# The u products' input in PSUM, the latents' sums in the scores' banks, and all of the context's v rows on VectorE

## The chip, the core and the metric

The kernel runs on one core of one Trainium2 chip. The metric is the time of one execution on the device in microseconds (us); less is better. A core has TensorE (PE in the profile; its weight loads are PEld), VectorE (DVE), ScalarE (ACT), GpSimd (POOL) and SyncE (SP), which run their own instruction streams side by side and wait for each other by semaphores. SBUF is the working memory; PSUM is the memory that TensorE writes its products to, here eight banks of 512 float32 per partition.

## What is computed

The reference is a two-layer diffusion backbone over 256 latent tokens and 256 context tokens of width 1024. Each layer mixes tokens (two attentions, a convolution, a pooling, four gated branches) and then runs a retrieval network on every token:

```
def chunk(xc):                      # 128 tokens
    q = (xc @ wq).reshape(128, 8, 2, 128)
    ...                             # top 16 of 256 candidates for each of 8 heads
    gate = softmax(sc)
    u = jnp.take(u_tab, idx, axis=0)                    # 128 rows of 1024 for each token
    act = gelu(jnp.einsum('td,thkd->thk', xc, u))
    v = jnp.take(v_tab, idx, axis=0)                    # another 128 rows
    return jnp.einsum('thk,thkd->td', gate * act, v)
```

So every token needs 128 rows of `u_tab`, a dot product with each, and a weighted sum of 128 rows of `v_tab`; all is float32. The context is needed only up to the first layer's end, so there are six chunks of 128 tokens: two of context (layer 1), two of latents (layer 1), two of latents (layer 2).

## The kernel before

A chunk is a tile of 128 tokens, one on each partition. Its gather runs over j = 0 to 127; for each j, `u_slot` has GpSimd issue an indirect DMA (line 1124) that brings one row of `u_tab` for each of the 128 tokens (512 KB), and VectorE multiplies it with the tile's input `h2` and sums along the row (line 1132, a scalar_tensor_tensor of 128x1024, "the u product"). Sixteen j make a group; after it, ScalarE and VectorE turn the group's 16 dot products into weights. `v_slot`, one group behind, issues the DMA of a v row and adds weight times row to a sum: either on VectorE into the SBUF tile `dacc` (line 1149, "the v sum"), or on TensorE, where ScalarE first makes a diagonal matrix `dg` of the weights (line 1154) and two float32 matmuls of 512 columns add the row to `va`, two PSUM banks (line 1156). At the end `add` (lines 1170, 1171) scales each sum and adds it to the residual `X`.

The six gathers run in this order, and the text calls them so: C0 (context, first tile), L0 and L1 (latents, layer 1), C1 (context, second tile), F0 and F1 (latents, layer 2). Which j's v rows VectorE sums is set by a rule for each (line 1272): C0 all but 6, L0 and F0 every fourth, L1 and F1 every second, C1 three in four but one. C0 runs beside the latents' token mixer of layer 1 and C1 beside that of layer 2: their rows are put between the mixer's products as `pump` gives them credit, in program order. L0, L1 and F1, and F0 after its first rows, run with nothing large beside them but the router of their neighbour, whose selections of the top 16 are VectorE's.

The rows land in places: SBUF buffers, 5 for u and 5 for v beside the mixers, 12 and 9 with those lent in layer 1's latents (`lend`). GpSimd waits where no place is free. `h2` is made by `prepare` (lines 1102 to 1113) from `X`, a scale and two rows that TensorE spreads over the partitions in PSUM tiles `tr`. `va` is one PSUM tile of two banks; `at`, two tiles of one bank each, holds the attentions' scores; `mm` and `tr` take the other four banks. Each engine's instructions stand in the order that a scheduler gave them at build time, and run in it.

## Time and profile before

| | us |
|---|---|
| median of 3 runs | 3176.56 |
| lowest, highest | 3165.32, 3186.99 |
| the profiled execution | 3168.74 |
| its span, first to last instruction | 3167.0 |

| engine | busy, us | share of the span |
|---|---|---|
| PE (matmul) | 2376.9 | 75% |
| DVE | 2357.8 | 74% |
| POOL | 1789.3 | 56% |
| ACT | 654.6 | 21% |

The profile is of one execution. A group of instructions is named by its line, engine and operation and by "output<-inputs" (an `h` there is `h2`, `u,act` the u product's outputs). [...] The indirect rows are 805.40 of the 1036.48 MB that the kernel moves. "issue" is time in which an engine waited for nothing that the profile shows.

### The profile page before, as it was taken

Reading aid. Unit: us, or ns where it says so; the run is one execution under the profiler, and the core shown is the slowest. Engines: PE = TensorE matmul, PEld = TensorE weight load, DVE = VectorE, ACT = ScalarE, POOL = GpSimd, SP = SyncE. Lnnn points to the kernel's source line nnn. Section 1 sums busy time; section 2 is a strip of 40 time slices with the busy share of each in tenths; the row PEclk is TensorE's granted clock in tenths of the full one; section 3 lists DMA queues with packets and bytes.
Section 4 is the critical chain, followed back from the end, with each engine's and each line's share of the span. In section 5 each row is a group of like instructions: output and inputs, shape, how many; then the busy total and the mean of one; then the engine's idle time right before and its main releaser. Section 6 shows DMA issues by size and latency. Waiting matters only on the chain.

```text
span 3167.0 us, 32196 instructions
## 1 busy us (share of the span) xinstructions
PE 2376.9 (75%) x10264; PEld 1586.2 (50%) x10264; DVE 2357.8 (74%) x5204; ACT 654.6 (21%) x1543; POOL 1789.3 (56%) x1542
## 2 busy tenths in 40 slices
PE   7999989898877785665455589899997966645555
PEld 5879878666666452222111267667696522211111
DVE  5977679678968899747666769977567985566666
ACT  3454321233112211110000211123332211100001
POOL 0000057443556687776777757766205777777775
PEclk9999999899988897886777789899998988876767
DMA  9948979787999899998999999999838989999998
GB/s 305 334 161 285 304 263 351 270 296 250 339 331 356 321 392 364 336 381 294 373 369 369 338 343 389 341 388 386 300 107 288 323 324 372 372 344 372 383 377 300
DMA packets 397863, 1036.48 MB, mean 327 GB/s; under 512 B 30464, under 2 KB 169216, under 8 KB 397696
## 3 DMA queue, kind: packets, MB, share of 16 engines
q0 software_dynamic: 221184, 805.40, 68.0%
q1 hardware_dynamic: 173072, 226.25, 21.0%
q10 hardware_dynamic: 3440, 2.78, 0.3%
q8 instruction: 82, 1.34, 0.2%
q14 instruction: 85, 0.70, 0.1%
HBM read 1032.22 MB, written 2.10 MB: 327 GB/s over the span
## 4 chain that ended last, share of the span: by engine, by line
PE 33%; DVE 18%; issue 17%; DMA 15%; POOL 15%; ACT 1%; another core or an unknown queue 0%; POOLq 0%; SPq 0%; ACTq 0%; DVEq 0%
PE mm L218 11%; POOL u L1124 8%; POOL v L1124 7%; DMA v<-in_v_dram,idx 7%; DVE u L1132 5%; PE va L1156 4%; DMA w<-in_w_gate_dram 3%; PE mm L214 3%; PE mm L216 2%; PE mm L215 2%; PE mm L916 2%; DMA u<-in_u_dram,idx 2%; DVE dacc L1149 2%; PE at L531 2%; DVE m L832 2%
## 5 line engine op out<-in xcount | busy, mean ns | idle before, releaser
L1124 POOL DMA_INDIRECT u<-in_u_dram,idx x768 | 869.7, 1132 | 926.4 <-DVE m L862 409.0
L1156 PE MATMUL va<-v,dg 128*128 128x512 f32 x1436 | 890.5, 763 | 554.5 <-DMA v<-in_v_dram,idx 379.8
L1132 DVE SCALAR_TENSOR_TENSOR u<-u,h 128x1024 f32<-128x1024 f32 x768 | 933.2, 1219 | 338.1 <-DMA u<-in_u_dram,idx 307.6
L1124 POOL DMA_INDIRECT v<-in_v_dram,idx x768 | 919.1, 1197 | 433.6 <-issue 193.9
L1156 PEld LDWEIGHTS va<-v,dg 128*128 128x128 f32 x1436 | 315.8, 237 | 1070.4 <-issue 925.6
L1149 DVE SCALAR_TENSOR_TENSOR dacc<-v,wt,dacc 128x1024 f32<-128x1024 f32 x403 | 515.6, 1279 | 105.9 <-DMA v<-in_v_dram,idx 78.6
L218 PE MATMUL mm<-hT,w 128*128 128x256 f32 (+1 forms) x1664 | 383.4, 385 | 71.4 <-DMA w<-in_w_gate_dram 50.9
L218 PEld LDWEIGHTS mm<-hT,w 128*128 128x128 f32 x1664 | 312.4, 207 | 130.2 <-issue 53.6
L1154 ACT ACTIVATE dg<-ident,wt 128x128 f32<-128x128 f32 x359 | 141.3, 400 | 1029.9 <-PE va L1156 524.7
L832 DVE SCALAR_TENSOR_TENSOR m<-m,cols,m 128x256 f32<-128x256 f32 x360 | 158.2, 473 | 0.1
L916 PE MATMUL mm<-hT,w 128*128 128x256 f32 x512 | 134.5, 405 | 14.5 <-DVE t L453 6.6
L215 PE MATMUL mm<-hT,whi 128*128 128x256 f32 x512 | 143.4, 280 | 0.0
L214 PE MATMUL mm<-hT,whi 128*128 128x256 f32 x448 | 128.0, 286 | 3.1 <-ACT whi L176 3.1
L216 PE MATMUL mm<-hT,whi 128*128 128x256 f32 x448 | 127.2, 284 | 1.8 <-DVE whi L177 1.8
L218 PE MATMUL mm<-w,hT 128*128 128x256 f32 x512 | 117.1, 388 | 10.6 <-DMA w<-in_w_in_dram 10.6
L916 PEld LDWEIGHTS mm<-hT,w 128*128 128x128 f32 x512 | 97.6, 202 | 34.5 <-issue 17.2
L177 DVE TENSOR_TENSOR whi<-w,whi 128x1024 fp32r<-128x1024 f32 x86 | 103.6, 1220 | 13.8 <-ACT whi L176 6.5
L218 PEld LDWEIGHTS mm<-w,hT 128*128 128x128 f32 x512 | 99.1, 195 | 26.4 <-issue 12.5
L176 ACT CAST whi<-w 128x1024 fp32r<-128x1024 f32 x86 | 87.4, 1047 | 51.3 <-PE mm L216 20.6
L215 PEld LDWEIGHTS mm<-hT,whi 128*128 128x128 f32 x512 | 97.0, 190 | 0.4 <-issue 0.3
L214 PEld LDWEIGHTS mm<-hT,whi 128*128 128x128 f32 x448 | 85.3, 190 | 8.8 <-ACT whi L176 4.2
L216 PEld LDWEIGHTS mm<-hT,whi 128*128 128x128 f32 x448 | 84.8, 189 | 7.2 <-DVE whi L177 3.7
(361 smaller groups left out, 2960.9 us busy)
## 6 DMA issues: line engine op xcount, KB each, us to landing
w<-in_w_gate_dram SPq DMA_DIRECT2D x48, 1024.0 KB
w<-in_w_in_dram SPq DMA_DIRECT2D x42, 1024.0 KB
X<-in_w_mod_dram SPq DMA_DIRECT2D x40, 512.0 KB
wm<-in_w_mod_dram SPq DMA_DIRECT2D x40, 512.0 KB
w<-in_w_branch_dram SPq DMA_DIRECT2D x20, 1024.0 KB
w<-in_w_q_dram SPq DMA_DIRECT2D x20, 1024.0 KB
u<-in_u_dram,idx POOLq DMA_INDIRECT x768
v<-in_v_dram,idx POOLq DMA_INDIRECT x768
```

Of the source, the lines that this page charges most:

```text
L177: nc.vector.tensor_tensor(lo.bitcast(FR), v, hi, op=OP.subtract)
L214: nc.tensor.matmul(ps, ah, bh, start=first, stop=False)
L215: nc.tensor.matmul(ps, ah, bl, start=False, stop=False)
L216: nc.tensor.matmul(ps, al, bh, start=False, stop=last)
L218: nc.tensor.matmul(ps, a[:, kb, ca], b[:, kb, cb], start=first, stop=last)
L832: nc.vector.scalar_tensor_tensor(acc[:, b, :], yb[:, b, k:k + T], cols[:, l, cw + k:cw + k + 1], acc[:, b, :], op0=OP.mult, op1=OP.add)
L916: nc.tensor.matmul(ps, a[:, kb, ca], b[:, k0 + kb, cb], start=f, stop=z, skip_group_check=True)
L1124: nc.gpsimd.indirect_dma_start(out=r, out_offset=None, in_=table, in_offset=bass.IndirectOffsetOnAxis(ap=self.idx[:, j:j + 1], axis=0))
L1132: nc.vector.scalar_tensor_tensor(r, r, 1.0, self.h2, op0=OP.mult, op1=OP.mult, accum_out=self.act[:, j % 16:j % 16 + 1])
L1149: nc.vector.scalar_tensor_tensor(self.dacc, v, w, self.dacc, op0=OP.mult, op1=OP.add)
L1154: nc.scalar.activation(dg, ident, AF.Copy, scale=w)
L1156: nc.tensor.matmul(self.va[:, half, :], dg, v[:, half * 512:(half + 1) * 512], start=j == self.pe[0], stop=j == self.pe[-1])
```

## The change

`prepare` computes `h2` in SBUF as before up to its last step; for a tile of latents (t > 1) the last addition writes into a PSUM tile of the tag `va`, and the u products read that. The tile's sums on TensorE go to two tiles of the tag `at`. A context tile has no rows on TensorE any more: `self.pe` is empty, VectorE sums all 128, and `add` runs once. The rules for C0 and C1 fall away.

```
         def prepare(self, found=False):
 
-            self.h2 = sb.tile([128, D], F, tag="h2", name="h2", bufs=2)
+            h2 = sb.tile([128, D], F, tag="h2", name="h2", bufs=2)
+
+            self.h2 = va_ps() if self.t > 1 else h2
             if found:
-                nc.vector.tensor_copy(self.h2[:, ::512], self.idx[:, :2])
+                nc.vector.tensor_copy(h2[:, ::512], self.idx[:, :2])
             for half in range(2):
                 c = slice(half * 512, (half + 1) * 512)
                 ps = bcast(tr_ps(), A[self.l][1][:, self.s, half * 4:half * 4 + 4])
-                nc.vector.scalar_tensor_tensor(self.h2[:, c], X[:, self.t, c], rst2[:, self.t:self.t + 1], ps,
+                nc.vector.scalar_tensor_tensor(h2[:, c], X[:, self.t, c], rst2[:, self.t:self.t + 1], ps,
                                                op0=OP.mult, op1=OP.mult)
                 ps = bcast(tr_ps(), modc[self.l][:, self.s, 24 + half * 4:28 + half * 4])
-                nc.vector.tensor_tensor(self.h2[:, c], self.h2[:, c], ps, op=OP.add)
+                nc.vector.tensor_tensor(self.h2[:, c], h2[:, c], ps, op=OP.add)
 
         def begin(self, on_dve):
 
-            self.pe = [j for j in range(128) if not on_dve(j) or j >= 128 - LAST]
+
+            self.pe = [j for j in range(128) if not on_dve(j) or j >= 128 - LAST] if self.t > 1 else []
             self.dv = [j for j in range(128) if j not in self.pe]
-            self.va = va_ps().rearrange("p (a b) -> p a b", a=2)
+            self.va = [at_ps() for half in range(2)] if self.pe else None
...
-                    nc.tensor.matmul(self.va[:, half, :], dg, v[:, half * 512:(half + 1) * 512],
+                    nc.tensor.matmul(self.va[half], dg, v[:, half * 512:(half + 1) * 512],
                                      start=j == self.pe[0], stop=j == self.pe[-1])
...
-        t.add(t.va.rearrange("p a b -> p (a b)"))
+        if t.pe:
+            t.add(t.va)
...
-    P_C0, P_L0, P_L1, P_C1, P_F0, P_F1 = (lambda j: j < 48 or (j * 15) % 16 < 15), few, half, most, few, half
+    P_L0, P_L1, P_F0, P_F1 = few, half, few, half
...
-    behind.append(gather(tsc[0], P_C0, None, rc))
+    behind.append(gather(tsc[0], None, None, rc))
...
-    behind.append(gather(tsc[1], P_C1))
+    behind.append(gather(tsc[1], None))
```

Line numbers of the changed kernel are higher by 2 to 4 (the u product is line 1135 there, the v sum 1152, `add` 1173 and 1174, `prepare` 1112 and 1115).

VectorE at the hand-over from L0 to L1, before: L0's last v sums, its two `add`s (the sum in `dacc`, then the one in `va`) and L1's first u products, with L1's input `h_9901`, which was made earlier.

```order
L1149 SCALAR_TENSOR_TENSOR dacc<-v,wt,dacc 128x1024 x4
L1170 TENSOR_TENSOR dacc<-dacc,g_9926 128x512 x2
L1171 TENSOR_TENSOR X<-X,dacc 128x512 x2
L1132 SCALAR_TENSOR_TENSOR u,act<-u,h_9901 128x1024
L1170 TENSOR_TENSOR dacc<-va,g_9926 128x512 x2
L1171 TENSOR_TENSOR X<-X,dacc 128x512 x2
L1132 SCALAR_TENSOR_TENSOR u,act<-u,h_9901 128x1024 x5
```

And now (`h_9880` is L1's input before its last step, `h_11154` that of C1):

```order
L1135 SCALAR_TENSOR_TENSOR u,act<-u,va 128x1024 x3
L1115 TENSOR_TENSOR va<-h_9880,tr 128x512
L1142 TENSOR_TENSOR wt<-wt,gate 128x16
L1115 TENSOR_TENSOR va<-h_9880,tr 128x512
L1152 SCALAR_TENSOR_TENSOR dacc<-v,wt,dacc 128x1024 x2
L1112 SCALAR_TENSOR_TENSOR h_11154<-X,few_cols,tr 128x512
L1152 SCALAR_TENSOR_TENSOR dacc<-v,wt,dacc 128x1024
L1115 TENSOR_TENSOR h_11154<-h_11154,tr 128x512
L1152 SCALAR_TENSOR_TENSOR dacc<-v,wt,dacc 128x1024
L1173 TENSOR_TENSOR dacc<-dacc,g_9906 128x512 x2
```

The single tile `va` is written for L1 right behind L0's last u product; nothing else of the order at this place is new but C1's `prepare`, which moved up by a few instructions.

VectorE in C1, beside the convolution of layer 2 (line 832, a chain of 128x256 operations), before:

```order
L1132 SCALAR_TENSOR_TENSOR u,act<-u,h_11173 128x1024
L832 SCALAR_TENSOR_TENSOR m_11926<-m_11425,cols,m_11926 128x256
L1132 SCALAR_TENSOR_TENSOR u,act<-u,h_11173 128x1024
L832 SCALAR_TENSOR_TENSOR m_11926<-m_11425,cols,m_11926 128x256
L1149 SCALAR_TENSOR_TENSOR dacc<-v,wt,dacc 128x1024
```

And now:

```order
L1135 SCALAR_TENSOR_TENSOR u,act<-u,h_11154 128x1024
L832 SCALAR_TENSOR_TENSOR m_11888<-m_11405,cols,m_11888 128x256
L1152 SCALAR_TENSOR_TENSOR dacc<-v,wt,dacc 128x1024
L832 SCALAR_TENSOR_TENSOR m_11888<-m_11405,cols,m_11888 128x256
L1135 SCALAR_TENSOR_TENSOR u,act<-u,h_11154 128x1024
```

Every u product is now followed by a v sum. From the convolution's first instruction in C1 to its last there stood 27 v sums on VectorE and stand 34 now.

TensorE at the end of that stretch (line 916: the gates' products; `t_`: transposes of the attention's inputs; line 796: the convolution's statistics), before:

```order
L218 MATMUL mm<-w,hT 128x256 x13
L1156 MATMUL va<-v,dg 128x512 x2
L916 MATMUL mm<-hT,w 128x256
L463 MATMUL tr<-ident,t_12309 128x128 x4
L916 MATMUL mm<-hT,w 128x256 x14
L463 MATMUL tr<-ident,t_12372 128x128 x4
L916 MATMUL mm<-hT,w 128x256 x9
L1156 MATMUL va<-v,dg 128x512 x2
L796 MATMUL tr<-few_cols,m_11926 128x1 x3
```

And now:

```order
L218 MATMUL mm<-w,hT 128x256 x15
L916 MATMUL mm<-hT,w 128x256
L463 MATMUL tr<-ident,t_12256 128x128 x4
L916 MATMUL mm<-hT,w 128x256 x14
L463 MATMUL tr<-ident,t_12316 128x128 x4
L916 MATMUL mm<-hT,w 128x256 x9
L796 MATMUL tr<-few_cols,m_11888 128x1 x3
```

The context's v rows are gone from TensorE's order; the mixer's products stand as before.

## Rows read from the trace of the kernel before

**Rows 1.** The page's head: span and number of instructions.
```profile
span 3167.0 us, 32196 instructions
```
**Rows 2.** Stretches: us, busy (count) of PE, PEld, DVE, ACT, POOL; clock, DMA share, GB/s.
```profile
400.00:1000.00 600.00, 504.63 (x2342) 409.35 (x2342) 492.76 (x1110) 135.40 (x318) 318.91 (x256) 0.91 0.86 307
1040.00:1280.00 240.00, 175.50 (x499) 95.16 (x498) 235.46 (x781) 45.15 (x106) 186.38 (x151) 0.85 0.96 360
1280.00:1406.00 126.00, 83.55 (x160) 33.37 (x160) 77.09 (x137) 17.15 (x43) 98.59 (x86) 0.82 0.95 347
1440.00:1783.00 343.00, 190.93 (x286) 67.95 (x287) 230.92 (x332) 31.61 (x82) 264.48 (x242) 0.71 0.97 366
1784.00:2260.00 476.00, 414.05 (x1804) 314.12 (x1802) 371.08 (x652) 100.10 (x248) 323.77 (x256) 0.92 0.96 357
2440.00:2600.00 160.00, 126.53 (x414) 72.15 (x413) 153.50 (x503) 35.71 (x84) 110.02 (x96) 0.92 0.88 313
2600.00:2784.00 184.00, 123.52 (x231) 48.43 (x232) 93.29 (x138) 24.07 (x60) 134.36 (x129) 0.83 0.97 368
2790.00:3150.00 360.00, 185.61 (x249) 60.21 (x248) 239.66 (x342) 29.52 (x76) 272.87 (x252) 0.70 0.97 368
```
**Rows 3.** Waits in 1440 to 1783: us in total, times, longest.
```profile
POOL v L1124 <- issue: 36.3, 119, 0.3
...
DVE u L1132 <- DMA u<-in_u_dram,idx: 76.6, 57, 2.7
```
**Rows 4.** Timeline in F1: start, duration, engine, line, operation [idle before].
```profile
2899.78 0.94 POOL L1124 DMA_INDIRECT u<-in_u_dram,idx  x1 [0.30 <-issue]
...
2900.94 1.22 DVE L1132 SCALAR_TENSOR_TENSOR u<-u,h 128x1024 f32<-128x1024 f32 x1 [2.37 <-DMA u<-in_u_dram,idx]
2901.02 1.95 POOL L1124 DMA_INDIRECT v<-in_v_dram,idx  x1 [0.31 <-issue]
```
**Rows 5.** Timeline at the start of L1, beside `prepare`'s operation with a PSUM input.
```profile
1440.46 0.74 DVE L1110 SCALAR_TENSOR_TENSOR h<-X,few_cols,tr 128x512 f32<-128x512 f32 x1
1440.50 0.93 POOL L1124 DMA_INDIRECT u<-in_u_dram,idx  x1 [0.30 <-issue]
```
**Rows 6.** Line 1132 alone in L0's end, L1, F1: DVE busy (count); clock, DMA.
```profile
1280.00:1406.00 126.00, 52.14 (x86) 0.82 0.95 347
1440.00:1783.00 343.00, 150.26 (x246) 0.71 0.97 366
...
2790.00:3150.00 360.00, 157.25 (x256) 0.70 0.97 368
```
**Rows 7.** Line 1149 alone in the same stretches.
```profile
1280.00:1406.00 126.00, 16.67 (x13) 0.82 0.95 347
1440.00:1783.00 343.00, 78.36 (x61) 0.71 0.97 366
...
2790.00:3150.00 360.00, 78.32 (x61) 0.70 0.97 368
```
**Rows 8.** A stretch of F1, all engines.
```profile
3040.00:3080.00 40.00, 23.30 (x33) 7.52 (x32) 28.21 (x40) 3.02 (x8) 30.58 (x31) 0.74 1.03 408
```
**Rows 9.** Two lines: duration ns min/median/max, first and last start, form.
```profile
L1110 DVE SCALAR_TENSOR_TENSOR h<-X,few_cols,tr x12: 720/740/749, 414.4 to 2549.9; 128x512 f32<-128x512 f32 x12
...
L304 DVE SCALAR_TENSOR_TENSOR msum<-wm,silc,msum x28: 733/744/748, 106.8 to 353.7; 128x512 f32<-128x512 f32 x28
```
**Rows 10.** The page's group of line 1149: count | busy us, mean ns | idle before, releaser.
```profile
L1149 DVE SCALAR_TENSOR_TENSOR dacc<-v,wt,dacc 128x1024 f32<-128x1024 f32 x403 | 515.6, 1279 | 105.9 <-DMA v<-in_v_dram,idx 78.6
```
**Rows 11.** Two stretches of C1, all engines.
```profile
1920.00:2045.00 125.00, 108.47 (x431) 82.56 (x431) 121.19 (x225) 11.75 (x27) 93.71 (x66) 0.89 0.97 356
2045.00:2260.00 215.00, 207.70 (x959) 153.85 (x957) 151.96 (x247) 67.60 (x169) 141.09 (x118) 0.97 0.97 370
```
**Rows 12.** Line 1156 alone in the second of them: PE busy (count), PEld busy (count).
```profile
2045.00:2260.00 215.00, 32.38 (x64) 12.18 (x64) 0.97 0.97 370
```
**Rows 13.** The chain that ended last, in the same stretch, by line.
```profile
by line: PE mm L916 30.6%; DMA v<-in_v_dram,idx 14.8%; PE va L1156 10.6%; PE tr L218 9.7%; PE at L531 8.8%; PE tr L557 7.7%; DMA w<-in_w_gate_dram 5.5%; issue 4.6%; PE tr L553 3.9%; POOL v L1124 1.5%; POOL u L1124 1.1%; PE tr L1176 0.9%; PE
```

More of the change, by code (lines that the diff above doesn't have):

```diff
@@ L1150, in v_slot @@
                 if j == self.dv[-1]:
-                    self.add(self.dacc)
+                    self.add([self.dacc[:, :512], self.dacc[:, 512:]])
             else:
@@ L1169, in add @@
                 c = slice(half * 512, (half + 1) * 512)
-                nc.vector.tensor_tensor(self.dacc[:, c], v[:, c], self.g2[:, c], op=OP.mult)
+                nc.vector.tensor_tensor(self.dacc[:, c], v[half], self.g2[:, c], op=OP.mult)
                 nc.vector.tensor_tensor(X[:, self.t, c], X[:, self.t, c], self.dacc[:, c], op=OP.add)
```

## The prediction

> **What bounds the kernel now.** I first read the busy times by stretch, cut where a gather begins or ends and where its router stops [rows 2]. The kernel has no single bound. From 400 to 1000 us (C0) and from 1784 to 2260 (C1) the mixers' products on TensorE share the core with a gather. The stretches 1040 to 1280 (most of L0) and 2440 to 2600 (the first part of F0) carry the router's selections, and VectorE is busy for 235.46 of 240 and 153.50 of 160 us: it sets their time. Four stretches are left in which only a gather runs: 1280 to 1406 (L0's end), 1440 to 1783 (L1), 2600 to 2784 (F0's end) and 2790 to 3150 (F1), together 1013 us, a third of the span [rows 1].
>
> In these four no compute engine is full: VectorE is busy 51 to 67%, TensorE 52 to 67%. The DMA engines show a share of 0.95 to 0.97 and would pass for the bound. The second view, GpSimd's waits, says otherwise. Between two of its indirect DMAs lie 36.3/119 = 0.305 us of "issue", a wait for nothing shown, and hardly any other wait [rows 3]. L1 has 242 of them: 264.48 busy + 242 x 0.305 = 338 of 343 us. F1: 272.87 + 76.9 = 350 of 360. F0's end: 134.36 + 39.3 = 174 of 184; L0's end: 98.59 + 26.2 = 125 of 126 [rows 2]. GpSimd is never free there, and VectorE waits for its rows (76.6 us in L1) [rows 3]. It is the bound: a row costs its instruction's time plus 0.305 us.
>
> The third view is the timeline, for how long that instruction takes. Beside an idle VectorE it takes 0.94 us. One that starts 0.08 us after a u product, which reads two tensors from SBUF, takes 1.95: the product ends at 2900.94 + 1.22 = 2902.16, and the DMA instruction 0.81 us later [rows 4]. Beside an operation of the same kind whose second tensor is in PSUM (`prepare`'s line 1110), it takes 0.93 [rows 5]. So GpSimd stands still behind a VectorE operation with two SBUF tensors, and not behind one with a PSUM tensor. For the latents the change turns the first into the second.
>
> **The cost of each part.** (1) The waits of GpSimd in the four stretches. Over 0.94 us an instruction: L0's end 98.59 - 86 x 0.94 = 17.8 us; L1 264.48 - 227.5 = 37.0; F0's end 134.36 - 121.3 = 13.1; F1 272.87 - 236.9 = 36.0 [rows 2]; in all 104. They stand behind u products and v sums, which both read two SBUF tensors; I split them by the busy times of the two: u products have 52.14 of 68.81 in L0's end, 150.26 of 228.62 in L1, 157.25 of 235.57 in F1 [rows 6, 7], so 76, 66 and 67%; for F0's end, with L0's rule for v rows, 76%. That makes 13.5 + 24.3 + 9.9 + 24.0 = 72 us behind u products and 32 behind v sums. The 72 fall away. But GpSimd then comes round sooner and meets v sums that it missed while it stood behind a u product: I let the 32 grow by a third, by 11. Net 61, and as GpSimd fills 97% of these stretches, 59 us. The bounds: 72 if the v sums catch no more than now, about 20 if they catch most of it. A row would then cost 1.34 us in place of 1.42; 1.29 us a row and less is seen already, in 40 us of F1 with 31 rows at 408 GB/s [rows 8], so the transfers can follow.
>
> (2) The same waits where VectorE is the bound: 186.38 - 141.9 = 44 us in L0's first stretch, 20 in F0's [rows 2]. VectorE idles there for only 4.5 and 6.5 us, so GpSimd merely fills its places earlier; of the 11 us I take 5. Bounds: 0, and 15 with what the filled places save behind the selections.
>
> (3) The u product from PSUM. No row shows a 128x1024 one. The nearest are the 128x512 operations of the same kind, 740 ns with a PSUM input and 744 without [rows 9]: no difference, so 0. [...]
>
> (4) The context's v rows. VectorE gets 6 + 33 = 39 v sums of 1.279 us [rows 10], 50 us, and loses two second `add`s. In C1 it is full from 1920 to 2045 (121.19 of 125) [rows 11], beside the convolution; 7 of the new sums fall there by the order: 9 us on the path. From 2045 to 2260 TensorE is full (207.70 of 215) [rows 11] and VectorE is not; the v rows take 32.38 us of TensorE [rows 12] and, with their transfers that it waits for in order, 25% of the chain, some 55 us [rows 13]. All that goes, but the transfers run at 370 GB/s already [rows 11]: at about 400, between that and the 408 of rows 8, the stretch would be 199 us, 16 less; I take 14. So C1 gains 5; bounds: 9 lost, 15 gained. In C0, 6 rows change engine, and neither engine is full (505 and 493 of 600) [rows 2]: 0, at worst 6 x 1.28 = 8 us.
>
> (5) `va` and `at`. The order writes `va` for the next tile right behind the last u product on the same engine, and the sums' tiles are handed on by the `add`, as `va` was: 0. Were the input late, 16 u products of the first group would be queued behind it, and with them GpSimd once its places are full: a few us at each of four hand-overs.
>
> Sum: -59 - 5 + 0 - 5 = -69 us against the profiled execution's 3168.74 (its span of 3167.0 and 1.7 around it): 3100. The median of the runs is 7.8 above that execution: 3107.
>
> **The rivals.** *The transfers are the bound.* For it: the DMA share of 0.95 to 0.97 [rows 2]. Then GpSimd's gain only lengthens the queue, and 3% of 1013 us, 30, is all there is: 3147. Against it: 408 GB/s where GpSimd was rarely held [rows 8]. [...] *The v sums take over.* VectorE runs v sums in 13% (L0's end) to 23% (L1) of a stretch [rows 7]; if GpSimd falls into step with them, only part (1)'s lower bound of 20 comes, with (2) and (4) 30: 3147. For it: half the rows of L1 and F1. *The PSUM operand doesn't free GpSimd*, because something else about the products holds it: only (4), 3172. Against it: rows 5, in the same kind of operation. *All waits shrink.* If fewer collisions also break up those behind v sums, 72 + 15 + 15 = 102 and more: 3070. *The other side: C1 starves.* With 128 v sums, u products and the convolution all reading two SBUF tensors, GpSimd may find no gap; it waits 83 us in C1 now and uses 402 of 476 with the pauses [rows 2]. Its time must pass 476 before this costs anything; and for the kernel to be slower by 1% C1 must grow by 64 (the gain of (1) and (2)) + 32 = 96 us. VectorE alone does not do it: 371 + 42 = 413 of 476 [rows 2]. Every wait would have to triple: 83 x 2 = 166, less the 74 of slack, 92 us, and the convolution's 9: 101, which gives 3177 - 64 + 101 = 3214.
>
> **How the numbers follow.** The forecast (a gain of 40 to 95 us, 3082 to 3137) 0.58; all waits shrink 0.12; the transfers 0.10; the v sums 0.10; no effect 0.04; C1 starves 0.06. One per cent, about what a measurement of this kernel can tell from no change, is 32 us: faster below 3145, slower above 3208. Forecast, larger gain and a third of the two rivals around 3147 are faster, 0.76; the rest of these and no effect are the same, 0.18; C1 is slower, 0.06. The range 3062 to 3158 leaves out half of the larger gain, the tail of the 3147s, no effect and C1: 2 in 10.
>
> **What would show it.** Right: in the changed kernel's L1 and F1, GpSimd's instruction takes about 1.01 us on average (now 264.48/242 = 1.09), those beside u products 0.94; the four stretches together come to about 950 us at 385 to 395 GB/s; the u product stays at 1.22 us. In C1 the convolution's stretch is longer by some 10 us and TensorE's after it shorter. Wrong: GpSimd's instructions at 0.94 but GB/s unchanged (the transfers); the mean unchanged with more of the long ones beside line 1152 (the v sums); still 1.9 us beside line 1135 (no effect); C1 over 500 us (starved).

## The result, and the profile after

The change made the kernel 1.6% slower where it was first timed: 3212.7 us (median of 4 runs, 3206.59 to 3224.56) against 3170.9 of the kernel before on the same chip, a ratio of 1.016 [1.013, 1.020]. The prediction was 3107 us. Repeated on two more chips it gave 1.0136 [1.0105, 1.0166] and 0.9882 [0.9837, 0.9928]: its sign differs from chip to chip, and the second half of the study is about that. Each chip was used on one occasion only, so chip and occasion aren't told apart.

The profiled execution after has a span of 3210.0 us, 43 more than before. The lines of it that answer to [rows 1, 2, 8, 11], in the same columns (cut where its gathers begin and end):

```profile
span 3210.0 us, 31926 instructions
```
```profile
1320.00:1422.00 102.00, 72.05 (x155) 29.48 (x154) 59.24 (x90) 15.52 (x38) 70.97 (x71) 0.86 0.97 365
1440.00:1791.00 351.00, 173.56 (x259) 60.47 (x260) 229.88 (x333) 31.08 (x81) 245.36 (x241) 0.70 0.95 361
...
1924.00:2061.00 137.00, 92.49 (x387) 75.88 (x386) 137.00 (x246) 8.51 (x19) 75.64 (x71) 0.83 0.91 338
2061.00:2293.00 232.00, 198.31 (x912) 155.69 (x912) 173.76 (x271) 62.88 (x157) 140.99 (x117) 0.87 0.92 344
...
2480.00:2640.00 160.00, 109.33 (x317) 58.61 (x315) 144.14 (x452) 30.46 (x72) 91.55 (x92) 0.87 0.82 299
2640.00:2831.00 191.00, 126.91 (x247) 50.75 (x248) 96.91 (x145) 25.14 (x63) 128.48 (x132) 0.82 0.96 366
2836.00:3191.00 355.00, 181.66 (x251) 59.46 (x249) 236.43 (x342) 27.71 (x73) 253.98 (x253) 0.72 0.97 374
```

The four gather-only stretches come to 102 + 351 + 191 + 355 = 999 us where they were 1013 [rows 2], at 361 to 374 GB/s; forecast were 950 at 385 to 395. (The cut in L0, where its router stops, lies at 1280 us before and at 1320 now, in a gather that starts 15 us later; the table by gather below is the safer measure.) GpSimd's instruction did get shorter as forecast: 245.36/241 = 1.018 us in L1 and 253.98/253 = 1.004 in F1. Beside a u product that reads PSUM it takes 0.94 us, where it took 1.95 beside one that read SBUF [rows 4] (timeline in F1):

```profile
2855.22 1.22 DVE L1135 SCALAR_TENSOR_TENSOR u<-u,va 128x1024 f32<-128x1024 f32 x1
2855.79 0.94 POOL L1127 DMA_INDIRECT u<-in_u_dram,idx  x1 [0.30 <-issue]
```

Over all of L1 and F1, GpSimd's instructions that start during a u product took 1.36 and 1.28 us in the mean before and take 0.94 in both now; those that start during a v sum, which still reads two SBUF tensors, took 1.15 and 1.19 and take 1.29 and 1.24.

The u product itself costs the same from either memory (line 1135 by form: duration min/median/max in ns):

```profile
L1135 DVE SCALAR_TENSOR_TENSOR u<-u,va x512: 1192/1217/1223, 1021.2 to 3172.5; 128x1024 f32<-128x1024 f32 x171
...
L1135 DVE SCALAR_TENSOR_TENSOR u<-u,h x256: 1175/1218/1277, 416.9 to 2267.0; 128x1024 f32<-128x1024 f32 x128
```

But GpSimd is no longer busy throughout. Its waits in L1 (us in total, times, longest), where before, beside the pauses of [rows 3], there was one of over 0.3 us:

```profile
POOL v L1124 <- remote: 5.4, 1, 5.4
```
and after:
```profile
POOL v L1127 <- issue: 42.0, 113, 4.6
POOL u L1127 <- issue: 32.7, 107, 0.4
POOL v L1127 <- remote: 12.8, 4, 5.1
POOL v L1127 <- DVE dacc L1150: 8.5, 1, 8.5
```

By gather, from the first u issue to the last v issue (us; "between" is from C1's end to F0's start):

| | C0 | L0 | L1 | C1 | between | F0 | F1 |
|---|---|---|---|---|---|---|---|
| before | 574.5 | 403.2 | 376.2 | 473.4 | 119.1 | 406.8 | 364.7 |
| after | 588.9 | 404.9 | 369.3 | 500.6 | 112.7 | 424.9 | 358.5 |
| change | +14 | +2 | -7 | +27 | -6 | +18 | -6 |

Sum: +42 of the 43. So there are three questions: where the gain of L1 and F1 is, and what made C1 (with C0) and F0 longer. For the first, GpSimd's time in L1 and F1 in three parts: its 256 instructions, the pauses between them (up to 0.31 us each), and all other waits (us, summed from its timeline; the second chip is the one numbered 7 below):

| | instructions | pauses | other waits | in all |
|---|---|---|---|---|
| L1 before, after | 279.2, 259.2 | 77.5, 77.5 | 19.3, 32.3 | 376.2, 369.3 |
| F1 before, after | 276.5, 256.6 | 77.5, 77.4 | 10.5, 24.2 | 364.7, 358.5 |
| chip 7: L1 before, after | 269.9, 255.6 | 77.5, 77.5 | 0.0, 0.1 | 347.6, 333.5 |
| chip 7: F1 before, after | 285.0, 250.0 | 77.5, 77.5 | 0.0, 2.0 | 362.7, 329.8 |

On the first chip GpSimd's own work fell by 40 us in the two, and its other waits grew by 27.

### The profile page after: what moved, and what is told of

It reads as the page before. It is cut to its first block, busy times and chain, and to the rows that moved or that the text cites. A ratio compares the mean times of both kernels' runs of the same rounds, so it can differ in the third digit from the quotient of the medians.

```text
span 3210.0 us, 31926 instructions
## 1 busy us (share of the span) xinstructions
PE 2295.7 (72%) x10108; PEld 1562.5 (49%) x10108; DVE 2391.3 (74%) x5235; ACT 638.6 (20%) x1504; POOL 1643.0 (51%) x1542
## 4 chain that ended last, share of the span: by engine, by line
PE 33%; DVE 22%; issue 16%; DMA 12%; POOL 10%; another core or an unknown queue 4%; ACT 2%; SPq 1%; ACTq 0%; POOLq 0%; DVEq 0%
PE mm L218 11%; DVE u L1135 7%; POOL v L1127 6%; PE at L1159 5%; DMA v<-in_v_dram,idx 4%; POOL u L1127 4%; DVE dacc L1152 4%; DMA w<-in_w_gate_dram 4%; PE mm L214 3%; PE mm L216 2%; PE mm L916 2%; PE mm L215 2%; DVE m L832 2%; PE at L531 2%
## 5 line engine op out<-in xcount | busy, mean ns | idle before, releaser
L1127 POOL DMA_INDIRECT u<-in_u_dram,idx x768 | 814.9, 1061 | 1053.5 <-DVE m L862 407.9
L1159 PE MATMUL at<-v,dg 128*128 128x512 f32 x1280 | 778.7, 755 | 515.8 <-DMA v<-in_v_dram,idx 224.2
L1127 POOL DMA_INDIRECT v<-in_v_dram,idx x768 | 827.5, 1078 | 495.6 <-issue 189.5
L1135 DVE SCALAR_TENSOR_TENSOR u<-u,va 128x1024 f32<-128x1024 f32 x512 | 617.4, 1215 | 224.6 <-DMA u<-in_u_dram,idx 193.4
L1159 PEld LDWEIGHTS at<-v,dg 128*128 128x128 f32 x1280 | 279.8, 234 | 982.4 <-issue 851.4
L1152 DVE SCALAR_TENSOR_TENSOR dacc<-v,wt,dacc 128x1024 f32<-128x1024 f32 x442 | 566.5, 1282 | 84.9 <-DMA v<-in_v_dram,idx 63.4
L1135 DVE SCALAR_TENSOR_TENSOR u<-u,h 128x1024 f32<-128x1024 f32 x256 | 311.7, 1219 | 16.7 <-DMA u<-in_u_dram,idx 15.8
L1157 ACT ACTIVATE dg<-ident,wt 128x128 f32<-128x128 f32 x320 | 125.3, 400 | 979.9 <-PE at L1159 349.8
L215 PEld LDWEIGHTS mm<-hT,whi 128*128 128x128 f32 x512 | 97.4, 190 | 0.4 <-issue 0.3
L214 PEld LDWEIGHTS mm<-hT,whi 128*128 128x128 f32 x448 | 85.7, 191 | 8.7 <-ACT whi L176 4.2
```

The source lines that it names most:

```text
L214: nc.tensor.matmul(ps, ah, bh, start=first, stop=False)
L215: nc.tensor.matmul(ps, ah, bl, start=False, stop=False)
L1127: nc.gpsimd.indirect_dma_start(out=r, out_offset=None, in_=table, in_offset=bass.IndirectOffsetOnAxis(ap=self.idx[:, j:j + 1], axis=0))
L1135: nc.vector.scalar_tensor_tensor(r, r, 1.0, self.h2, op0=OP.mult, op1=OP.mult, accum_out=self.act[:, j % 16:j % 16 + 1])
L1152: nc.vector.scalar_tensor_tensor(self.dacc, v, w, self.dacc, op0=OP.mult, op1=OP.add)
L1157: nc.scalar.activation(dg, ident, AF.Copy, scale=w)
```

## The experiments

They ran on five chips, which the records of the runs number 13, 5, 12, 4 and 7; that of the first comparison has no number there and may be one of them. Each ratio is against the kernel before on the same chip. "Theory 1" in the expectations says that the context's v rows on VectorE cost C0 and C1 their time; "theory 2" that TensorE's rows end late and hold the latents' gathers; "theory 8" that the rate at which rows arrive does.

**The change in parts (chip 13).** The context's v rows alone, on the kernel before (code cut to the lines that matter, here and below):

```
-            self.pe = [j for j in range(128) if not on_dve(j) or j >= 128 - LAST]
+            self.pe = [j for j in range(128) if not on_dve(j) or j >= 128 - LAST] if self.t > 1 else []
...
-    behind.append(gather(tsc[1], P_C1))
+    behind.append(gather(tsc[1], None))
```

> The kernel before with one part of the change alone: all 128 v rows of the two context tiles on VectorE, their one add with them. The latents keep their input in SBUF and their sums in the tile of rows' sums. Theory 1 (the context's rows are what cost): the traces give C0 589 us after against 575, and C1 501 against 473; then this kernel has the same two, about 35 us in all (C0 +14, C1 +27, and 6 of it given back before F0), and a ratio of about 1.011. Theory 2 (the loss comes from the latents, through TensorE's rows whose end is seen late): C0 and C1 change by under 10 us together, ratio 0.998 to 1.003. The prediction on record said -5 for this part.

1.0086 [1.0051, 1.0122]; C0 588.1, C1 495.6, the other four within 6 us of before. The latents' sums in the scores' banks alone:

```
-            self.va = va_ps().rearrange("p (a b) -> p a b", a=2)
+            if self.t > 1:
+                self.va = [at_ps() for half in range(2)]
...
```

> The kernel before with one part of the change alone: the latents' sums stand in two tiles of the scores' banks in place of the one tile of rows' sums; the input of the u products stays in SBUF, the context's rows stay on TensorE. Theory 3 (the new place of the sums itself makes waits): F0 longer by about 18 us as in the changed kernel, ratio 1.005 or more. Theories 1 and 2: no difference that can be measured, ratio 0.997 to 1.003, each gather within 6 us of before.

0.9995 [0.9964, 1.0026]: the banks cost nothing that the time shows, though the gathers of the one trace differ more than I expected (L0 395.4, F1 379.1 us). The whole change with C1's rows back on TensorE:

```
...
-    P_L0, P_L1, P_F0, P_F1 = few, half, few, half
+    P_L0, P_L1, P_C1, P_F0, P_F1 = few, half, most, few, half
...
-    behind.append(gather(tsc[1], None))
+    behind.append(gather(tsc[1], P_C1))
```

> The changed kernel with C1's v rows put back on TensorE by the old rule (every fourth one), their sums in the tile of rows' sums; C0 and the latents as in the changed kernel. Theory 1: C1 is back at about 473 us, the time falls by some 22 to 27 us against the changed kernel (3213 to about 3188, ratio to before 1.004 to 1.007). Theory 2: the latents keep their loss and C1 matters little: about 3205 to 3215, ratio 1.012 to 1.015.

1.0077 [1.0050, 1.0105], C1 469.2: C1 is back at its old time, though the kernel isn't. The 0.8% left are half of the first comparison's loss, but the changed kernel itself wasn't timed on this chip; with four `dg` buffers (below) it was at 1.0106. F0 stays at 426.1, L1 and F1 at 365.3 and 359.1. That the context's rows cost C1 its time (theory 1) holds; the context's rows alone gave 1.0082 [1.0055, 1.0108] on chip 12, with C0 585.5 and C1 496.4:

> The context's v rows alone on VectorE, as in e1, beside the other three. If C1's loss is the full VectorE and its queue in order, and not the chip, C1 is again 20 to 28 us longer than in the kernel before on either chip, and the ratio 1.006 to 1.012.

**F0's order (chips 5 and 12).** VectorE's order of the changed kernel lets two of the router's selections (line 1011 and what follows) go ahead of F0's second 16 u products: ahead of u products 0, 4, 8, ... of F0 there stand 0, 5, 6, 6, 22, 30, 30 of its maxima (lines 1011 and 1014, twelve to a selection), before 0, 5, 6, 6, 6, 6, 22, 30. Those 16 take 60 to 64 us where they took 39 to 41, and VectorE's queue waits at the first selection (waits in 2438 to 2502 of after):

```profile
DVE mx L1011 <- ACT sc L1202: 12.9, 1, 12.9
```

F0 alone with its input in SBUF, on the changed kernel, and that with C1's rows back:

```
-            self.h2 = va_ps() if self.t > 1 else h2
+            self.h2 = va_ps() if self.t > 1 and (self.t, self.l) != (2, 1) else h2
```

> The changed kernel, but F0 alone takes the input of its u products from SBUF as before. In every kernel with F0's input in PSUM so far the second 16 u products of F0 take 60 to 62 us in place of 40, because two selections stand ahead of u products 16 to 27 on VectorE; here they stand behind them again, as in the kernel before. Theory 6 (F0 lost its 18 us to this order): F0 falls from 425 to 405 to 411 us, the kernel by some 15 against the changed one, ratio to before about 1.006 to 1.011. If reading PSUM itself slows F0, only its first groups change and F0 stays over 418.

> The changed kernel with its two losses taken back: C1's v rows on TensorE by the old rule, and F0's input of the u products in SBUF; L0, L1 and F1 keep the input in PSUM. By the parts so far C1 falls by 24 us and F0 by 16: on a chip of the second kind ratio 0.975 to 0.985, the best of all; on one of the first kind 0.997 to 1.005.

The order is as before in both, the second 16 take 39 us again, and the same wait is 0.6 us in 2374 to 2413 of the first. F0 is 394.1 (chip 5) and 405.1 us (chip 12; 429.8 in the changed kernel on that chip). The ratios are 0.9902 [0.9865, 0.9940] and 1.0009 [0.9991, 1.0028]. Both costs, C1's and F0's, are gone in the second, and still nothing is gained on chip 12: the five gathers other than C0 are 14 us shorter together than in the kernel before on that chip, and C0, whose rows stay on VectorE, is 24 longer (591.0 against 567.1). The first, for which I expected 1.006 to 1.011, gains a per cent on chip 5 though C1's 490.1 us stand in it: that miss is what led to the question of the chips.

**TensorE's rows that end late.** In L1 and F1 of after, ScalarE waits up to 10 us longer for TensorE's rows than to their ends as the profile models them. Its wait for a place for `dg`, and the row that uses the other place, by the timeline (TensorE's row ends at 2708.35, ScalarE starts at 2719.46):

```profile
2719.46 0.40 ACT L1157 ACTIVATE dg<-ident,wt 128x128 f32<-128x128 f32 x1 [10.10 <-remote]
```
```profile
2706.40 1.95 PE L1159 MATMUL at<-v,dg 128*128 128x512 f32 x4 [0.60 <-DMA v<-in_v_dram,idx]
```

Counted from the modelled end of the row two back or the start of ScalarE's idle time, whichever is later, such waits of over 2 us come to 395 us in after and 185 in before (the expectations' count, 425 and 220, was a little wider). The runs that try whether they are the bound: four `dg` buffers in place of two (chip 13); TensorE's rows of L1 and F1 left out in both kernels (all but the first and the last are gathered and not summed), and four filler products behind each row of L1 and F1 (all chip 4):

```
+                if self.t > 1 and self.pe.index(j) % 2:
+                    dg = sb.tile([128, T], F, tag="th", name="dg", bufs=2)[:, :128]
...
```
```
-            else:
+            elif self.t < 3 or j in (self.pe[0], self.pe[-1]):
```
```
+                if self.t == 3:
+                    spare = mm_ps()
+                    for n in range(4):
+                        nc.tensor.matmul(spare[:, :256], dg, cs.rearrange("p a b c -> p (a b c)"), start=n == 0, stop=n == 3)
```

> The changed kernel with four buffers in place of two for the scaled identity that ScalarE makes for each v row of TensorE (two of them in places that only the first layer's mixers use). ScalarE may then run four rows ahead of TensorE's last finished row in place of two. In the changed kernel's trace ScalarE waits in 69 of the latents' 320 rows for over 2 us longer than to the modelled end of the row that it follows (425 us in all, before 43 rows and 220 us), up to 10.8 us each, and a late row holds a v place and with it GpSimd. Theory 2 (this chain took back what GpSimd gained): the waits over 2 us fall to a third or fewer and the latents' four gathers, 1558 us, lose 40 to 60: about 3155 to 3175, ratio 0.995 to 1.002. Theory 1: the latents change by under 10 us, ratio 1.013 to 1.018.

> The kernel before; in L1 and F1 (the second latent tile of each layer) the v rows of TensorE are gathered as before, but only the first and the last of them are scaled and summed: the sums leave out the 62 others. Every transfer and every VectorE operation stays. Theory 2 (on chips of the first kind TensorE's late ends hold v places and with them GpSimd): GpSimd is the bound, 1.08 + 0.305 = 1.39 us a row, L1 and F1 350 to 360 us. Theory 8 (those chips' transfers are slower): both stay at 365 to 376.

> The changed kernel with the same rows left out of the sums of L1 and F1. Theory 2: also on a chip of the first kind L1 and F1 come to 331 to 337 us, about 405 GB/s, as e7 and e8 show on the other chip; the kernel some 60 us below the changed one. Theory 8: 359 to 370 us and at most 377 GB/s as in the changed kernel.

> The changed kernel; in L1 and F1 four more 128x256 matmuls follow each v row on TensorE, into a spare bank that nobody reads, so that TensorE is busy for nearly twice as long. If the late ends belong to a TensorE that idles between its rows, the waits of ScalarE over 2 us (14 and 18 in L1 and F1 of the changed kernel, 220 us) fall to under 40 us and L1 and F1 to 331 to 345. If not, they stay or grow, and L1 and F1 are 360 us or more. On a chip without late ends: 331 to 340, no difference.

With four buffers L1 and F1 took 369.8 and 359.9: nothing (1.0106 [1.0069, 1.0143]). ScalarE is late by the row two back for 119 us only, but it waits there for the row four back, and by that row it is late for 350: the run spares TensorE a wait and leaves the late ends. Without TensorE's rows L1 and F1 took 361.5 and 366.5 in the kernel before and 362.1 and 356.6 in the changed one (0.9993 [0.9970, 1.0017] and 1.0104 [1.0068, 1.0140]). GpSimd's other waits fell to 0.0 and 0.2 us in the one and to 14.4 and 12.7 in the other, so TensorE's rows have a part in them; but its instructions got longer, 1.11 and 1.13 us in the one and 1.06 and 1.04 in the other, and the time stayed. The filler took the late waits of L1 and F1 from 214 us in after to 155 and added time (382.5 and 374.7 us; 1.0193 [1.0154, 1.0233]). Theory 2 falls: TensorE's rows alone aren't what holds L1 and F1.

**Transfers out of the way (chip 5).** Both kernels with the latents' rows gathered half as wide (512 of 1024 columns, each used twice, so the sums are others):

```
+            w = 512 if self.t > 1 else D
+            table = table.rearrange("n (h c) -> (n h) c", c=w)
...
+            nc.gpsimd.indirect_dma_start(out=r[:, D - w:], out_offset=None, in_=table,
```

> The kernel before, the latents' rows gathered half as wide: each indirect DMA brings 128 half rows of 2 KB (other rows than the real ones) into the right half of a place, and the products, sums and matmuls read that half twice, so that every engine does the work that it did and the transfers half of it. What the latents add is not the reference's. Theory 4 (the latents' steady part is bound by the transfers: 1.41 us a row at about 372 GB/s in all kernels so far, GpSimd's instruction at 1.08 or 1.00): L1 and F1 fall from 376 and 365 us to about 350, where GpSimd's 1.08 + 0.305 us a row binds, 1.39 us. Theory 5 (something on the core binds, TensorE's late ends and the v places that they hold): L1 and F1 stay within 6 us.

> The changed kernel with the same half-wide rows for the latents; what they add is not the reference's. Theory 4: with the transfers out of the way what the change gave GpSimd shows: its 1.00 + 0.305 = 1.31 us a row, L1 and F1 at about 330 to 340 us, 15 to 20 shorter than the kernel before with half rows. Theory 5: no difference between the two, L1 about 369 and F1 about 359 as with whole rows.

Half rows were slower than whole ones, which I had not expected: GpSimd's instruction grew to 1.20 and 1.21 us in L1 and F1 (before) and to 1.09 and 1.06 (after), so my numbers missed. What holds is the comparison, of one execution each: with GpSimd's instructions and pauses at 98 to 100% of both, L1 went from 415.3 to 389.3 us and F1 from 422.0 to 381.1. Where GpSimd is the bound the PSUM input gains 26 and 41 us.

**PSUM input for L1 and F1 alone (chips 5 and 4).** The kernel before, with the sums in the scores' banks and the input in PSUM for the latents' second tile only:

```
-            self.h2 = sb.tile([128, D], F, tag="h2", name="h2", bufs=2)
+            h2 = sb.tile([128, D], F, tag="h2", name="h2", bufs=2)
+            self.h2 = va_ps() if self.t == 3 else h2
...
```

> The kernel before with the sums of the latents in the scores' banks and the input from PSUM for the second latent tile alone (L1 and F1, where no selections run); context, L0 and F0 as before. Theory 4: the transfers bind, so L1 and F1 gain about 6 us each as in the changed kernel (369 and 359 against 376 and 365), ratio 0.994 to 1.000. The prediction on record had 48 us for these two, ratio 0.985.

> The kernel of e8 once more (context, L0 and F0 as before, PSUM input in L1 and F1 alone). On a chip of the first kind L1 and F1 gain 3 to 6 us each: ratio 0.995 to 1.001. On one of the second kind 0.985 to 0.992 again.

Chip 5: 0.9885 [0.9843, 0.9926], L1 333.4 and F1 332.7 us (I expected 0.994 to 1.000). Chip 4: 0.9947 [0.9923, 0.9971], 363.2 and 361.5. It is the only version measured on both kinds of chip that was faster than the kernel before on both.

**Both unchanged kernels on other chips (12 and 7).**

> The kernel before once more, for a trace of its own on the chip of this comparison. The runs so far came from two chips: on one (e1 to e4; the profile of before is like it) the latents' steady part moves 367 to 377 GB/s in every kernel, and the end of a TensorE group is often signalled up to 10 us after the matmul's modelled end; on the other (e5 to e8) e7 and e8 move 403 to 408 GB/s and no end is late. Theory 7 (the chip's transfers and late ends decided): on a chip of the second kind this kernel is bound by GpSimd, L1 and F1 at about 350 us and 1.36 to 1.40 us a row; on one of the first kind 365 to 376 us and 1.41 as before.

> The changed kernel once more, beside the kernel before on the same chip. Theory 7: on a chip of the second kind L1 and F1 are at 331 to 335 us (1.28 us a row, GpSimd always busy), L0 about 380, F0 still 15 longer than with its input in SBUF, C0 and C1 together 35 to 40 longer than before: ratio 0.990 to 1.000; on a chip of the first kind 1.012 to 1.020 again. Were the chip no matter, the ratio is 1.016 on both.

> The kernel before, unchanged, for its trace beside the changed kernel's on one chip. If the transfers' rate decides in L1 and F1 (theory 8): on a chip whose rows come at 363 to 377 GB/s in the steady part, L1 and F1 of before take 365 to 376 us, as so far; on a chip where they come at over 400, GpSimd binds, its instruction takes 1.05 to 1.08 us, so a row 1.36 to 1.40 us, L1 and F1 350 to 360 us. If GpSimd decides everywhere: the same 365 to 376 us on any chip.

> The changed kernel, unchanged, on the same chip. Theory 8: on a chip at 363 to 377 GB/s L1 and F1 take 358 to 372 us and the ratio is 1.013 to 1.020; on a chip at over 400 GB/s they take 330 to 335 us, some 40 to 50 us less in both together than so far, and the ratio is 0.998 to 1.006, with C1 (about 495 us) and F0 (about 420) as long as elsewhere. If GpSimd decides everywhere: the ratio is 1.013 to 1.020 on any chip.

On chip 12 the result repeats (1.0136; L1 and F1 371.8 and 361.1 us against 370.6 and 365.2). On chip 7 the changed kernel takes 3076.5 us against 3116.8, 0.9882 [0.9837, 0.9928]; I expected 0.998 to 1.006 for a chip of its kind, and F0's loss did not come. L1 and F1 there, the kernel before and then the changed one (columns as in [rows 2]), and all but the smallest of GpSimd's waits in the changed one's L1:

```profile
1409.00:1755.00 346.00, 203.75 (x303) 69.61 (x301) 243.09 (x351) 33.14 (x86) 268.85 (x254) 0.67 1.00 386
2740.00:3100.00 360.00, 192.32 (x255) 61.50 (x256) 239.97 (x344) 29.75 (x76) 282.83 (x254) 0.68 0.98 369
```
```profile
1400.00:1732.00 332.00, 179.62 (x306) 62.98 (x305) 240.10 (x349) 33.78 (x87) 254.64 (x254) 0.79 1.02 400
2726.00:3054.00 328.00, 177.99 (x254) 57.56 (x253) 235.82 (x342) 28.66 (x74) 248.83 (x254) 0.76 1.02 405
```
```profile
POOL v L1127 <- issue: 35.1, 115, 0.3
POOL u L1127 <- issue: 34.8, 114, 0.3
```

GpSimd is never free in either: 268.85 + 254 x 0.305 = 346 of 346 us before, 254.64 + 77.5 = 332 of 332 after. This is the picture on which the prediction was made, and here its mechanism gives what it said for L1 and F1. Whether GpSimd or the transfers end the gain there can't be told: the DMA engines show 1.02, and no stretch of 30 us read in any run goes above some 410 GB/s.

The chips side by side; the rate is that of L1 and F1 between the issues of the 33rd and of the last row of u, in all kernels with whole rows (on chip 5 both have the PSUM input in L1 and F1):

| chip | before, median us | GB/s | kernels traced |
|---|---|---|---|
| of the first comparison | 3170.9 | 369 to 377 | before, after |
| 13 | 3167.8 | 357 to 376 | 4 |
| 12 | 3181.3 | 363 to 374 | 4 |
| 4 | 3163.4 | 363 to 375 | 4 |
| 5 | 3113.6 | 403 to 408 | 2 |
| 7 | 3116.8 | before 382, 396; after 405, 408 | 2 |

## Why the prediction was wrong

**Term (1), the four stretches: -59 predicted, -14 measured** (by gather: L1 and F1 -13, the ends of L0 and F0 from the 97th u row on -1 and +6). The cost in the term was right: net of the v sums it has 48.3 x 59/72 = 40 us for L1 and F1, and GpSimd's instructions there took 40 us less. The step that failed is the one behind it, that GpSimd stays never free and that the transfers can follow because a 40-us window ran at 408 GB/s [rows 8]: of the 40 us, 27 came back as waits of GpSimd for places. The window was one of two conditions between which each trace on four of the chips changes to and fro: smooth parts at some 410 GB/s, where a packet takes 159 to 172 ns, and disturbed ones at 300 to 360, where single packets take up to 1.9 us. Two windows of F1 in the changed kernel, and what the second moved in 40 slices of 0.75 us:

```profile
2840.00:2870.00 30.00, 4.54 (x7) 1.81 (x8) 26.83 (x45) 1.31 (x4) 22.69 (x25) 0.60 1.02 407
2885.00:2915.00 30.00, 13.36 (x18) 4.53 (x17) 18.22 (x27) 1.60 (x5) 17.47 (x19) 0.73 0.90 340
```
```profile
GB/s 421 410 399 421 404 410 410 415 399 421 410 410 404 421 404 399 421 404 404 421 404 410 410 415 404 388 82 0 120 333 300 229 360 279 289 262 393 180 38 87
```

The mean over both conditions is what [rows 2] show as 366 to 368 GB/s, and a GpSimd that is ready earlier doesn't raise it. So L1 and F1 came out as the rival of the transfers had it; I gave it one in ten, because I took the best 40 us of a 360-us stretch for what the stretch can do. Its mechanism, full transfers, is not shown: where the rate falls to 0 above, the DMA engines have nothing to do, because GpSimd issues no row for 4 us: by 2905.5 every row issued has been moved. GpSimd, ScalarE, TensorE and VectorE all stand still and go on within 0.7 us of each other:

```profile
2899.43 0.94 POOL L1127 DMA_INDIRECT u<-in_u_dram,idx  x1 [0.30 <-issue]
2904.55 0.94 POOL L1127 DMA_INDIRECT v<-in_v_dram,idx  x1 [4.18 <-remote]
```
```profile
2904.38 0.40 ACT L1157 ACTIVATE dg<-ident,wt 128x128 f32<-128x128 f32 x1 [10.10 <-remote]
```

On chip 7 the term holds: L1 and F1 went from 347.6 + 362.7 to 333.5 + 329.8, 47 us less for 40. L0's and F0's ends gave nothing there (109 to 108 and 105 to 107 us): 16 rows of each table took 41 us in F0's end before already.

**Term (2): -5 predicted.** L0 gave +2 (on chip 7 -15), and F0 lost 18 by a cause that is not in the sum: the order. It could be read before the run, in the same listing of which three places are shown, but I priced only the places that I had chosen. Whether the 20 us of the second 16 u products come back differs with the chip again. In the third 16 (2500.3 to 2566.2 of after, then 2423.7 to 2477.5 on chip 7) VectorE has the same 54 us of work and idles for 12 in the one and not at all in the other:

```profile
2500.30:2566.20 65.90, 48.88 (x168) 29.56 (x167) 54.11 (x166) 11.57 (x28) 33.47 (x34) 0.90 0.80 303
```
```profile
2423.70:2477.50 53.80, 47.06 (x167) 27.87 (x165) 53.69 (x166) 11.86 (x28) 35.14 (x35) 1.00 0.96 366
```

So F0 is 389.5 us there against 388.3, and 424.9 against 406.8 here.

**Terms (3) and (5): right.** The u product took 1217 ns from PSUM and 1218 from SBUF (medians). The hand-over of `at` cost nothing that a run shows (the banks alone: 0.9995); that of `va` no run tests by itself.

**Term (4), the context: -5 predicted, +27 in C1 and +14 in C0 measured.** The convolution's stretch went from 131.4 to 136.9 us (+6; I said +9), and the 125 us ahead of it to 131. The step that failed is TensorE's stretch after it, which I let shrink by 14 because the v rows leave TensorE: it grew from 217.0 to 232.3 us (chip 7: 215.6 to 220.3). The v rows' 34 us of TensorE did go, but its idle time in the stretch rose from 8 to 34 us, and its other products took 198 us where they took 180 (912 records against 894), at a granted clock of 0.87 in place of 0.97: of the two levels that the traces record, 1.0 and 0.5, TensorE had the lower one for 61 us of it, before for 14. The stretch before, then the waits in 2061 to 2293 of after of VectorE, TensorE and GpSimd:

```profile
2040.00:2257.00 217.00, 209.14 (x962) 154.70 (x961) 151.45 (x247) 68.08 (x170) 143.68 (x121) 0.97 0.97 369
```
```profile
DVE st L838 <- PE tr L796: 16.7, 1, 16.7
```
```profile
PE mm L916 <- DMA w<-in_w_gate_dram: 11.9, 2, 11.5
```
```profile
POOL u L1127 <- DVE u L1135: 33.5, 7, 17.1
```

The long waits come from the order again. It is not so that the mixer's products stand as before on TensorE: later than the place shown ahead of the prediction, two of the gates' products, the first that read the next weights, moved ahead of the convolution's second statistics (line 796). Before:

```profile
2044.57 1.99 PE L916 MATMUL mm<-hT,w 128*128 128x256 f32 x8 [0.56 <-ACT t L931]
2046.40 1.17 PE L796 MATMUL tr<-few_cols,m 128*128 128x1 f32 x10
```

And after:

```profile
2061.42 1.99 PE L916 MATMUL mm<-hT,w 128*128 128x256 f32 x8 [0.56 <-ACT t L931]
2074.95 2.08 PE L916 MATMUL mm<-hT,w 128*128 128x256 f32 x4 [11.54 <-DMA w<-in_w_gate_dram]
2076.82 2.13 PE L796 MATMUL tr<-few_cols,m 128*128 128x1 f32 x10
```

In both kernels these weights are issued as the products before them end (2046.60 and 2063.45) and are there some 12 us later. Before, TensorE did the statistics, 7 us of other products and a v row meanwhile; now it waits 11.5 us, VectorE's queue stands behind the statistics, and GpSimd runs out of places behind VectorE. All ten traces with this order have 13 to 17 us of that wait of VectorE and a C1 of 489 to 501 us (517 with half rows); all ten without it have 2 to 5 us and 466 to 475 (499 with half rows). The order and the added v sums always went together, so their shares are not told apart. I had taken the transfers that TensorE waited for in the chain [rows 13] as time that vanishes with the rows, and had not looked for what would wait in their place. On chip 7 the same wait is 15.6 us, and C1 is 15 us longer (473.9 to 488.6).

C0 is 574.5 to 598.9 us in the twelve traces with all its rows on VectorE and 567.1 to 581.1 in the eight others, so the +14 of one pair of traces is not firm. Its seventh group of 16, though, takes 71 to 75 us in the twelve and 60 to 67 in the eight: VectorE waits 8 to 10 us for ScalarE there, at line 856, and in none of the eight.

The rival in which C1 starves gave 3214, nearly the measured time, and its sign, C1 over 500 us, was met, both by luck: GpSimd's instruction in C1 did not get longer (1.23 and 1.14 us for u and v rows, 1.22 and 1.31 before).

**The sum by chip.** First comparison: L1 and F1 -13, L0 +2, F0 +18, C0 and C1 +41, between -6: +42. Chip 7: -47, -15, +1, +21, and -6 for the rest: -46 of its span (3120.0 to 3073.8).

## What to carry to other kernels

A rate seen in the best 40 us of a trace is not what a stretch can hold: look for the share of the stretch that runs at that rate, and at who waits for whom in the rest, before a gain at the engine that issues the transfers is counted. An engine that gets faster can simply wait longer: here 40 us less work of GpSimd gave 13 us. An operand's place can move the order that a build-time scheduler gives an in-order queue far from the edit: read the whole difference of the order on the engine that binds, not only the places around the edit. Work taken out of a full queue lets what stood behind it move up, here two products whose weights were not there yet, with statistics that another queue needs behind them.

## What the runs showed of the hardware that was not expected

**Chips differ.** The same kernel takes 3114 to 3117 us on two chips and 3163 to 3181 on the others, rows come at up to 408 GB/s on the two and at 357 to 377 on the others, and one change is 1.2% faster on one of the two (chip 7) and 1.4 to 1.6% slower on two of the others.

**Signals come late on the four, not on the two.** TensorE's late ends above are one form: ScalarE's waits of over 2 us for them come to 395 us in the changed kernel of the first comparison and to 24 on chip 7, where L1 and F1 have none. VectorE's are another. In the changed kernel without TensorE's rows, 30 smooth and 30 disturbed us of L1, and VectorE's v sums in the second:

```profile
1546.00:1576.00 30.00, 0.00 (x0) 0.00 (x0) 21.46 (x32) 0.22 (x1) 22.72 (x24) 0.50 1.03 410
1660.00:1690.00 30.00, 0.00 (x0) 0.00 (x0) 16.84 (x25) 0.00 (x0) 20.85 (x19) 0.50 0.88 307
```
```profile
1672.30 1.28 DVE L1152 SCALAR_TENSOR_TENSOR dacc<-v,wt,dacc 128x1024 f32<-128x1024 f32 x1 [3.44 <-remote]
...
1679.30 1.28 DVE L1152 SCALAR_TENSOR_TENSOR dacc<-v,wt,dacc 128x1024 f32<-128x1024 f32 x1 [3.44 <-remote]
...
1686.30 1.28 DVE L1152 SCALAR_TENSOR_TENSOR dacc<-v,wt,dacc 128x1024 f32<-128x1024 f32 x1 [3.44 <-remote]
```

They start every 7.00 us, each after 3.44 us in which the engine is idle, and each 0.02 us after a recorded signal (1672.28, 1679.28, 1686.28) on a semaphore that only VectorE's own instructions raise. The row of the last one had been issued at 1662.66, and the signals of its arrival that the trace holds end at 1668.26, 18 us before the sum starts. On chip 7 the same semaphore rises 0.01 us after a v sum ends.

**Records go missing on the same chips.** For the 1,536 row transfers the traces of chips 5 and 7 hold 24,576 rises of the semaphores, 16 for each (24,574 in one trace), those of the four others 12,764 to 18,768, fewer in kernels with a PSUM input (12,764 to 14,416) than without (15,984 to 18,768). In each of the two windows of L1 shown last 43 signals of any kind are recorded in 30 us, one in 0.7 us in the mean, and the starts above are ten times that apart.

What stays open: whether the long packets, the late signals and the lost records have one cause, and which comes first. In the window shown last the rows are there and the engines idle, so late signals hold it and not the transfers; how much of the lost time that makes is not measured, because no run took VectorE's late signals away. Nothing was run that tells whether the recording itself delays the signals on these chips, nor what of the chip or the occasion (the tables' place in its memory, or other use of that memory, for two) makes the difference.
